# b, k and v of the RWKV pairs turned by VectorE and block moves instead of TensorE, the inverses' blocks packed, and row buffers taken later

## The chip, the cores and the metric

The kernel runs on one core of a Trainium2 chip. The metric is the device time of one execution in microseconds (us), as the median of several runs. A core has TensorE (PE in the profile; its weight loads are PEld), VectorE (DVE), ScalarE (ACT), GpSimd (POOL), SyncE (SP), which here issues every transfer, and 16 DMA engines.

## What is computed

One step of a hybrid decoder layer, for 1024 prompt tokens and 8 single-token samples with their own states, in float32:

```python
p = x @ w_in                                   # 1024 -> 9344 columns: GLA, RWKV, gates
p_gla, p_rwkv, p_gate = split(p)
o_gla, S_gla = gla_chunked(q, k, v, log_a)     # 4 heads, gated linear attention
pr = p_rwkv + (previous_token(p_rwkv) - p_rwkv) * mu
r, kb, vb, g_b, w_lr, aa_lr = split(pr)
...
# RWKV-7, 16 heads of 64, token after token:
S = S * w_t + (S @ -kk_t) (kk_t * a_t)^T + v_t k_t^T ;  y_t = S r_t
...
m = sigmoid(gate_a) * (o_gla @ w_up_gla) + sigmoid(gate_b) * (o_rwkv @ w_up_rwkv)
y = layernorm(ALPHA * x + m @ w_out)
```

The outputs are `y` for both groups and the new states.

## The kernel before

**Passes and blocks.** The tokens are worked in two passes: pass 0 has 512 prompt tokens and the 8 samples (two tiles of 260 columns), pass 1 the other 512 (one tile). Every projection is a list of blocks of 128 output columns. A block is 8 steps over the inner dimension, and each step three matmuls in a reduced format, with `x` and the weights split in a high and a low part (`xh`, `xl`, `whi`, `wlo`), added up in a PSUM bank of the group `proj` (two banks). In pass 0 the weights are loaded (`wraw`), split by ScalarE and an elementwise engine, and the parts are written to DRAM (`wh`, `wl`); pass 1 reads the parts back. `whi` and `wlo` have four buffers of half a block each, so there is room for the block at work and one more.

**Pairs.** The RWKV heads are worked in eight pairs per pass, 16 in all. Time is cut in `NCH` = 8 chunks of `C` = 64 tokens. Of a pair:

- `front` computes decays and the chunk's factors: `BK` (b and k, two heads by 64 tokens, for each chunk; a buffer of the group `wide`), `AZ` (a and r), and by matmul `GG`, the masked products of each chunk, whose part `GG[..., 0, h, ...]` is a strictly lower triangular 64 x 64 matrix per head.
- Each such matrix has an inverse that is built from 32 x 32 blocks. The diagonal blocks go to DRAM (`LD`) and come back with one matrix per partition (`L`, in a `wide` buffer); 31 pairs of VectorE operations solve them in `X`; they go to DRAM (`XD`) and back as blocks (`XT`).
- `back` computes the off-diagonal block: `X1` = `XT`'s first block transposed on VectorE, `pA` = `GG` x `X1`, copied to `As`, `pZ` = `As` x `XT`, copied to `XT`. Both are eight matmuls, one per chunk, on 128 x 128 weights with 64 columns, in float32, which the profile shows as two instructions each. Then `AZ` is copied into `GG`.
- `turn` transposes `BK` (eight 128 x 128 transposes on TensorE, four to a bank, each bank copied back over `BK`) and `v` (four, copied in four parts to `u`, which takes over `L`'s buffer). In the profile these are `big<-cons,wide` and `big<-cons,row`, since they run as matmuls with the identity in `cons`.
- `chain` goes through the 8 chunks one after the other, four dependent matmuls each, and `norm` finishes the pair.

There are buffers for two pairs at a time (`az`, `gg`, `XT` two each, `wide` four).

**Rows.** Results of a block go to a row buffer ([128, 520], 26 of them, the group `row`). In `blocks`, `evac = yield from b.act()` takes the row before the block's first matmul; the function it returns empties the bank later.

**Order.** The whole program is written out by a planner (`Order.run`): each piece of work is a stream, every operation has a price and a planned start, and at each step the operation with the smallest planned start less its stream's priority is issued. Each engine then runs its own list in that order; SP's list is one queue for all transfers. Streams of the kind `turn` have priority 0.5, those of the weights 0.3, and 0.6 more while no split weights are ready.

All operations are issued from one line of the planner's helper, line 215, so the profile tells them apart by their buffers: `big<-X,gg` is `pA`, `big<-XT,As` is `pZ`, `proj<-xh,whi` a projection.

Of the kernel before, what the change touches and what calls it, by code (L numbers as in the profile page):

```python
# [20 lines left out]
P = 128  # L21
# [28 lines left out]
    "sto": ([P, P], 1), "bnd": ([P, 1], 3), "st": ([P, 32], 3), "part": ([P, HALF], 2), "l2p": ([P, 2 * P], 2),  # L50
    "pair": ([P, 2, HT // 32], 3),
}
PARTS = ("part", "l2p")
# [349 lines left out]
class Kern(Order):  # L403
# [71 lines left out]
    def setup(self):  # L475
# [149 lines left out]
    def load_w(self):  # L625

        H = NK // 2
        todo = [(b.src, b.c0, j, b.c.i) for b in self.plan if b.src is not None for j in range(2)]
        raws, his, los, kept = [], [], [], {}

        def keep(src, c0, j, hi, lo):
            for v, x in zip("hl", (hi, lo)):
                t = self.dr.tile([P, 512], F32, name=f"w{v}{c0}_{j}")
                kept.setdefault((c0, j), []).append(t)
                yield self.S.dma_start(t, x.bitcast(F32))

        def high():
            n = 0
            while True:
                yield lambda: len(raws) > n  # L640
                hi = yield from self.get("whi")
                yield self.A.copy(hi, raws[n][0])
                his.append(hi)
                n += 1
                if n == count:
                    return

        def low():
            for n in range(count):
                yield lambda: len(his) > n  # L650
                lo = yield from self.get("wlo")
                raw, src, c0, j, i = raws[n]
                yield self.E.tensor_sub(lo, raw, his[n].bitcast(F32))
                self.free(raw)
                los.append(lo)
                if src is self.a["w_in"] and i == 0:
                    yield from keep(src, c0, j, his[n], lo)
                self.ws.append((his[n], lo))
            self.w_done = True
# [61 lines left out]
    def low_rank(self, c, raws, used):  # L721
# [26 lines left out]
            c.alr_ready += 1  # L748
        self.free(x_)

    def gla_row(self, c, rows, scale):
        x = yield from self.row(c.n, KEEP)
        rows.append(x)

        def ev(tt, t0, w, q):
            yield self.A.activation(x[:, t0:t0 + w], q, AF.Copy, scale=scale)
        return ev

# [177 lines left out]


    def lora(self, c):
        c.lraw = yield from self.row(c.n)
        return self.shift(c, 32, c.lraw, c.lraw[:, HT:])  # L940

    def lora_done(self, c):
        def parts():
# [40 lines left out]
    def shift(self, c, j, dst, smp):  # L984
# [4 lines left out]
        edge = {}  # L989

        def ev(tt, t0, n, q):
            np_ = n - c.ns if tt == last else n
            yield lambda: "pv" in self.has
            yield A.activation(dst[:, t0:t0 + n], q, AF.Copy, scale=omu)
            if tt < last:
# [12 lines left out]
                if not i:  # L1008
                    self.free(prev)
            if i == 0 and tt == last:  # L1010
                yield V.scalar_tensor_tensor(smp, self.shT[:, j], mu, dst[:, HT:c.n], ALU.mult, ALU.add)
        return ev

    def rwkv_row(self, c, rows, n, p):
        x = yield from self.row(c.n, KEEP)
        rows.append(x)
        return self.shift(c, 8 * n + p, x, self.smp[:, n, p])

    def pair(self, c, p, st, gate):
        d = SimpleNamespace()  # L1020
        yield lambda: len(self.idle["wide"]) > 1 and len(self.idle["az"]) > 0 and len(self.idle["gg"]) > 0 and c.fronts == p and c.lw_ready and "cst" in self.has
        yield from self.front(c, p, st, d)
        yield "turn"
        yield from self.back(d)
        yield from self.turn(d)
        yield "chain"
        yield lambda: self.chained == p - 1 + NPAIR * c.i
        yield from self.chain(c, p, d)
        self.chained += 1
        yield "norm"  # L1030
# [3 lines left out]
    def front(self, c, p, st, d):  # L1034
# [103 lines left out]
        d.AZ, d.BK, d.G, d.XT, d.v, d.bonus, d.pc, d.L = AZ, BK, GG, XT, st[2], st[1], pc, L_  # L1138
        d.y = Pc_[:, :HT]

    def back(self, d):
        GG, XT = d.G, d.XT

        X1_, As_ = (yield from self.get("X1")), (yield from self.get("As"))
        X1 = X1_.rearrange("p (c h t) -> p c h t", c=NCH, h=2)
        As = As_.rearrange("p (c h t) -> p c h t", c=NCH, h=2)
        q = [slice(32 * n, 32 * n + 32) for n in range(4)]
        for h in range(2):
            yield self.V.transpose(X1[q[2 * h], :, h], XT[q[2 * h], :, h, 0:32])
        pA = yield from self.bank("big", [P, NCH, 2, 32])  # L1150
        for x in range(NCH):
            yield self.P.matmul(pA[:, x], GG[:, x, 0], X1[:, x], start=True, stop=True)
        for h in range(2):
            yield self.C.copy(As[q[2 * h + 1], :, h, 0:32], pA[q[2 * h + 1], :, h])
        self.free(pA, X1_)
        pZ = yield from self.bank("big", [P, NCH, 2, 32])
        for x in range(NCH):
            yield self.P.matmul(pZ[:, x], As[:, x], XT[:, x, :, 32:64], start=True, stop=True)

        for h, hs in enumerate(HS):  # L1160
            yield self.C.copy(XT[q[2 * h], :, h, 32:64], pZ[q[2 * h], :, h])
            yield self.C.copy(GG[hs, :, 0, h], d.AZ[hs, :, 0, h])
        self.free(pZ, As_)

    def turn(self, d):

        for x in range(0, NCH, 4):
            pt = yield from self.bank("big", [P, 4, P])
            for n in range(4):
                yield self.tr(pt[:, n], d.BK[:, x + n])  # L1170
            yield self.C.copy(d.BK[:, x:x + 4], pt)
            self.free(pt)
        d.u = d.L.rearrange("p (c h v) -> p c h v", c=NCH, h=2)
        pt = yield from self.bank("big", [P, 4, P])
        for n in range(4):
            yield self.tr(pt[:, n], d.v[:, n * P:(n + 1) * P])
        self.free(d.v)
        for h in range(2):
            for n, hs in enumerate(HS):
                yield self.C.copy(d.u[HS[1 - h], n::2, h], pt[hs, :, h * C:h * C + C])  # L1180
        self.free(pt)

    def chain(self, c, p, d):
        A, V = self.A, self.V
# [171 lines left out]


    def gate_row(self, c, n, x):
        gt = yield from self.row(c.n, KEEP)

        def ev(tt, t0, w, q):
            yield self.A.copy(gt[:, t0:t0 + w], q)
            if tt == len(c.tiles) - 1:
                yield self.S.dma_start(self.sg[c.i][n][x], gt)
# [25 lines left out]
                    self.gts.append((gt, m))  # L1390

    def up_row(self, c, n, x):
        yield lambda: self.gts
        gt, m = self.gts.pop(0)

        def ev(tt, t0, w, q):
            s = slice(t0, t0 + w)
            yield self.V.tensor_mul(gt[:, s], q, gt[:, s])
            if n:
                yield self.E.tensor_add(gt[:, s], gt[:, s], m[:, s])  # L1400
# [189 lines left out]
    def run_all(self):  # L1590
# [4 lines left out]
        self.plan, self.xq, self.ws, self.wo, self.gts = [], [], [], [], []  # L1595
# [65 lines left out]
```

## Time and profile before

| what | us |
|---|---|
| median of three runs | 1655.22 |
| the runs | 1649.95, 1655.22, 1656.4 |
| span of the profiled execution, first to last instruction | 1647.8 |
| TensorE busy | 1604.5 (97%) |
| TensorE weight loads busy | 1422.9 (86%) |
| VectorE busy | 1234.7 (75%) |
| ScalarE busy | 844.6 (51%) |
| GpSimd busy | 103.3 (6%) |
| DMA engines, mean share of the span | 61.2% |

The profiled execution's whole device time isn't listed apart from the runs; its span is 2.2 us below the fastest of them and 7.4 below the median. How to read the rows: in groups of instructions, `out<-in` are the buffers, then partitions x elements, then the count; behind the first bar stand the busy time in us and the mean of one in ns, behind the second the idle time of the engine just before these instructions and what ended it. In a timeline the first column is the start, the second the duration, both in us. In the list of waits: the engine and what it wrote, `<-` what ended the wait, then us in total, times and the longest in us. SP's issues don't count as busy time. In rows by stage each engine has its busy time and instruction count, and the last three numbers are the granted TensorE clock, the DMA share and GB/s.

### The profile page before, as it was taken

The page shows a single profiled execution, that of the slowest core. Times are in us where ns is not written, and L with a number is a line of the kernel's source. Part 1 is how long each engine was busy: PE and PEld are TensorE (multiplying, and loading weights), DVE is VectorE, ACT ScalarE, POOL GpSimd, SP SyncE. Part 2 cuts the span into 40 slices and gives each one's busy share as a digit, 9 for nine tenths or more (in the row PEclk, how much of TensorE's full clock was granted, in tenths as well). Part 3 has the DMA queues.
Part 4 walks back from the last instruction along what each step waited for, and adds up shares of the span by engine and source line. Part 5 has one row for each costly group of instructions (what it writes and reads, how often), then busy time and mean ns, then how long its engine had stood idle before and what let it go on. Part 6 is the DMA issues. An engine that isn't in the chain of part 4 may idle for free.

```text
span 1647.8 us, 30094 instructions
## 1 busy us (share of the span) xinstructions
PE 1604.5 (97%) x10322; PEld 1422.9 (86%) x10322; DVE 1234.7 (75%) x3187; ACT 844.6 (51%) x2015; POOL 103.3 (6%) x192
## 2 busy tenths in 40 slices
PE   8999999999999999999999999999999999999998
PEld 7899999999999988788878787888788889988786
DVE  6787887788878887768678888796767775665565
ACT  5546755656476646553635462536345645554210
POOL 1100100100000000000001011100000000000000
PEclk9999999999999999999999999999999999999999
DMA  8878764696569655645465546544653577798432
GB/s 281 263 220 254 222 204 149 197 301 198 176 193 280 213 181 189 206 162 145 134 178 162 147 141 193 180 129 125 207 147 106 172 227 228 242 292 264 151 109 84
DMA packets 311925, 315.28 MB, mean 191 GB/s; under 512 B 75364, under 2 KB 197357, under 8 KB 311773
## 3 DMA queue, kind: packets, MB, share of 16 engines
q1 hardware_dynamic: 311772, 313.36, 61.2%
q8 instruction: 82, 1.34, 0.3%
q14 instruction: 71, 0.57, 0.1%
HBM read 195.45 MB, written 117.82 MB: 190 GB/s over the span
## 4 chain that ended last, share of the span: by engine, by line
PE 71%; DVE 13%; DMA 7%; ACT 3%; SPq 3%; issue 2%; POOL 0%; POOLq 0%; DVEq 0%; ACTq 0%
PE proj L215 39%; PE big L215 22%; PE pY L215 7%; PE pch L215 4%; DVE row L215 4%; SPq L215 3%; DVE X L215 2%; DVE Xt L215 2%; DMA wide<-LD 2%; ACT row L215 1%; DVE wide L215 1%; DVE wlo L215 1%; DVE pair L215 1%; DMA whi<-wh 1%; DMA l2s<-lora 1%
## 5 line engine op out<-in xcount | busy, mean ns | idle before, releaser
L215 PE MATMUL proj<-xh,whi 128*128 128x260 f32 (+1 forms) x1872 | 618.2, 330 | 0.1
L215 PE MATMUL proj<-xh,wlo 128*128 128x260 f32 (+1 forms) x1872 | 615.8, 329 | 0.5 <-POOL wlo L215 0.5
L215 PE MATMUL proj<-xl,whi 128*128 128x260 f32 (+1 forms) x1872 | 612.9, 327 | 0.8 <-DVE xl L215 0.7
L215 PEld LDWEIGHTS proj<-xh,wlo 128*128 128x128 f32 x1872 | 354.0, 189 | 28.0 <-issue 5.6
L215 PEld LDWEIGHTS proj<-xh,whi 128*128 128x128 f32 x1872 | 354.7, 189 | 24.7 <-issue 2.3
L215 PEld LDWEIGHTS proj<-xl,whi 128*128 128x128 f32 x1872 | 354.4, 189 | 24.8 <-issue 1.7
L215 ACT CAST whi<-wraw 128x512 fp32r<-128x512 f32 x210 | 130.1, 621 | 92.0 <-PE proj L215 42.3
L215 DVE TENSOR_TENSOR wlo<-wraw,whi 128x512 fp32r<-128x512 f32 x206 | 144.8, 706 | 42.1 <-ACT whi L215 37.3
L215 DVE TENSOR_TENSOR row<-row 128x512 f32<-128x512 f32 (+10 forms) x329 | 164.6, 505 | 11.5 <-PE big L215 4.5
L215 ACT ACTIVATE row<-row 128x512 f32<-128x512 f32 (+5 forms) x229 | 138.5, 610 | 33.2 <-DVE row L215 21.1
L215 ACT ACTIVATE row<-proj,omu 128x260 f32<-128x260 f32 (+1 forms) x99 | 54.2, 547 | 156.0 <-PE proj L215 155.6
L215 DVE TENSOR_TENSOR Xt<-X,wide 128x60 f32<-128x60 f32 (+24 forms) x496 | 108.7, 219 | 30.7 <-DMA wide<-LD 20.0
L215 PE MATMUL big<-row 128*128 128x64 f32 (+4 forms) x712 | 115.7, 281 | 6.5 <-DVE row L215 5.9
L215 DVE TENSOR_TENSOR X<-X,Xt 128x60 f32<-128x60 f32 (+24 forms) x496 | 107.4, 217 | 11.5
L215 ACT ACTIVATE s0p<-wide,pc 64x64 f32<-64x64 f32 x256 | 88.1, 344 | 43.4 <-DVE wide L215 39.1
L215 PEld LDWEIGHTS big<-row 128*128 128x128 f32 (+1 forms) x712 | 96.8, 191 | 15.5 <-DVE row L215 10.7
L215 DVE SCALAR_TENSOR_TENSOR wide<-pch,pc,s0p 64x64 f32<-64x64 f32 x224 | 63.1, 282 | 56.7 <-PE pch L215 52.2
L215 ACT COPY wide<-pch 64x64 f32<-64x64 f32 x230 | 47.3, 206 | 105.0 <-PE pch L215 101.6
L215 POOL TENSOR_TENSOR row<-row 128x512 f32<-128x512 f32 (+5 forms) x40 | 47.9, 1198 | 715.2 <-ACT row L215 210.8
L215 DVE SCALAR_TENSOR_TENSOR row<-proj,pv,row 128x259 f32<-128x259 f32 (+1 forms) x99 | 56.4, 570 | 40.5 <-ACT tail L215 23.7
L215 ACT COPY row<-big 128x128 f32<-128x128 f32 (+7 forms) x163 | 45.8, 307 | 52.4 <-PE big L215 51.3
L215 PE MATMUL big<-az,wide 128*128 128x256 f32 x256 | 66.7, 383 | 0.3 <-DVE gg L215 0.2
(256 smaller groups left out, 2714.5 us busy)
## 6 DMA issues: line engine op xcount, KB each, us to landing
wraw<-w_in SPq DMA_DIRECT2D x146, 256.0 KB
wh<-whi SPq DMA_DIRECT2D x146, 256.0 KB
wl<-wlo SPq DMA_DIRECT2D x146, 256.0 KB
whi<-wh SPq DMA_DIRECT2D x146, 256.0 KB
wlo<-wl SPq DMA_DIRECT2D x146, 256.0 KB
wide<-LD SPq DMA_DIRECT2D x64, 128.0 KB
wraw<-w_up_gla SPq DMA_DIRECT2D x32, 256.0 KB
wraw<-w_up_rwkv SPq DMA_DIRECT2D x32, 256.0 KB
```

The source lines that it names most:

```text
L215: ways.append((eng, lambda call=call: call(out, *args, **kw), price(eng, name, out, args, ins)))
```

## The change

- **b, k and v.** `turn` has no TensorE transposes any more. A new stream `turned`, started in `front` behind the `LD` and `Lp` transfers, transposes `v` and the two halves of `BK` in 32 x 32 blocks on VectorE into row buffers, frees `v`, writes the rows to DRAM (`VD`, `BD`), and reads `BD` back into `BK` in 16 block moves. `turn`, now ahead of `back`, reads `VD` into `u` in 8 moves. `chain` waits for `d.turned` as well, in the planner's order.
- **The inverses' blocks.** Four transfers gather the off-diagonal blocks of `GG` into `Lp`, in which four blocks stand on the diagonal of a 128 x 128 matrix; eight gather the solved blocks from `XD` into `Xs`. `back` then has four matmuls with 32 columns each for `pA` and for `pZ`, and eight copies of 32 partitions x 128 in place of four of 32 x 256.
- **Rows.** A block's row is taken by the new `landing`, in the function that empties the bank, with the first tile. `shift` gets a function `to` that is handed the row. `up_row` takes its place in the list `gts` at once and waits for the entry when it empties the bank.
- In `load_w` the line `los.append(lo)` moves behind the writes of the parts to DRAM.

```diff
+    "sto": ([P, P], 1), "Xs": ([P, 3 * P], 1), ...
+QS = tuple(slice(32 * n, 32 * n + 32) for n in range(4))
-        for tag, n, bufs in (("az", 4 * HT, 2), ("XT", 2 * HT, 2), ("X1", HT, 1), ("As", 2 * HT, 1)):
+        for tag, n, bufs in (("az", 4 * HT, 2), ("XT", 2 * HT, 2), ("Lp", HT, 1), ("As", HT, 1)):
...
-            evac = yield from b.act()
+            evac = b.act()
...
+    def landing(self, c, rows, tt):
+        if tt:
+            yield lambda: rows[0] is not None
+        else:
+            rows[0] = yield from self.row(c.n, KEEP)
+        return rows[0]
...
+        yield from self.turn(d)
         yield from self.back(d)
-        yield from self.turn(d)
         yield "chain"
-        yield lambda: self.chained == p - 1 + NPAIR * c.i
+        yield lambda: d.turned and self.chained == p - 1 + NPAIR * c.i
...
+        Lp = (yield from self.get("Lp")).rearrange("p (y t) -> p y t", t=P)
+        for n, b in enumerate(QS):
+            h = n % 2
+            yield self.S.dma_start(Lp[b, :, b], GG[QS[2 * h], n // 2::2, 0, h, 32:64])
+        VD = self.dr.tile([P, HT], F32, name=f"VD{c.i}{p}")
+        def turned():
+            BD = self.dr.tile([P, 2 * HT], F32, name=f"BD{c.i}{p}")
+            t = yield from self.row(HT)
+            yield V.transpose(t, v)
+            self.free(v)
+            yield self.S.dma_start(VD, t)
+            self.free(t)
+            for hf in range(2):
+                s = slice(hf * HT, hf * HT + HT)
+                t = yield from self.row(HT)
+                yield V.transpose(t, BK_[:, s])
+                yield self.S.dma_start(BD[:, s], t)
+                self.free(t)
+            src = BD.rearrange("(n a) (x q f) -> n q a x f", n=4, q=4, f=32)
+            for n, bn in enumerate(QS):
+                for q, bq in enumerate(QS):
+                    yield self.S.dma_start(BK[bq, :, bn], src[n, q])
+            d.turned = True
+        d.turned = False
+        self.spawn(turned(), "turn")
...
+        Xs = yield from self.get("Xs")
+        xp = Xs[:, :2 * P].rearrange("p (q y t) -> p q y t", q=2, t=32)
+        for n, b in enumerate(QS):
+            for q in range(2):
+                u = (2 * q + n % 2) * NCH + n // 2
+                yield self.S.dma_start(xp[b, q], XD[u:(2 * q + n % 2 + 1) * NCH:2].rearrange("c s t -> s c t"))
...
     def back(self, d):
-        for h in range(2):
-            yield self.V.transpose(X1[q[2 * h], :, h], XT[q[2 * h], :, h, 0:32])
-        for x in range(NCH):
-            yield self.P.matmul(pA[:, x], GG[:, x, 0], X1[:, x], start=True, stop=True)
...
+        yield self.V.transpose(d.Xs[:, 2 * P:3 * P], d.Xs[:, 0:P])
+        pA = yield from self.bank("big", [P, NCH // 2, 32])
+        for y in range(NCH // 2):
+            yield self.P.matmul(pA[:, y], d.Lp[:, y], X1[:, y], start=True, stop=True)
+        for b in QS:
+            yield self.C.copy(As[b, :, b], pA[b])
...
+        for y in range(NCH // 2):
+            yield self.P.matmul(pZ[:, y], As[:, y], X2[:, y], start=True, stop=True)
+        for n, b in enumerate(QS):
+            yield self.C.copy(XT[QS[2 * (n % 2)], n // 2::2, n % 2, 32:64], pZ[b])
...
     def turn(self, d):
-        for x in range(0, NCH, 4):
-            pt = yield from self.bank("big", [P, 4, P])
-            for n in range(4):
-                yield self.tr(pt[:, n], d.BK[:, x + n])
-            yield self.C.copy(d.BK[:, x:x + 4], pt)
-        for n in range(4):
-            yield self.tr(pt[:, n], d.v[:, n * P:(n + 1) * P])
...
+        src = d.VD.rearrange("(h n a) (x q f) -> h n q a x f", h=2, n=2, q=2, f=32)
         for h in range(2):
+            for n in range(2):
+                for q in range(2):
+                    yield self.S.dma_start(d.u[QS[2 - 2 * h + q], :, h, 32 * n:32 * n + 32], src[h, n, q])
```

More of the change, by code (lines that the diff above doesn't have):

```diff
@@ L49 @@
     "Xt": ([P, P], 1), "S": ([P, GDV], 2), "s0p": ([P, C], 2), "rh": ([P, P], 2),
-    "sto": ([P, P], 1), "bnd": ([P, 1], 3), "st": ([P, 32], 3), "part": ([P, HALF], 2), "l2p": ([P, 2 * P], 2),
+    "sto": ([P, P], 1), "Xs": ([P, 3 * P], 1), "bnd": ([P, 1], 3), "st": ([P, 32], 3), "part": ([P, HALF], 2), "l2p": ([P, 2 * P], 2),
     "pair": ([P, 2, HT // 32], 3),
@@ L749, in low_rank @@
         self.free(x_)
+    def landing(self, c, rows, tt):
[4 more added lines that the diff above has]
+        return rows[0]
     def gla_row(self, c, rows, scale):
-        x = yield from self.row(c.n, KEEP)
-        rows.append(x)
+        at = [None]
         def ev(tt, t0, w, q):
+            x = yield from self.landing(c, at, tt)
+            if not tt:
+                rows.append(x)
             yield self.A.activation(x[:, t0:t0 + w], q, AF.Copy, scale=scale)
@@ L938, in lora, with to @@
     def lora(self, c):
-        c.lraw = yield from self.row(c.n)
-        return self.shift(c, 32, c.lraw, c.lraw[:, HT:])
+        def to(x):
+            c.lraw = x
+        return self.shift(c, 32, to, None)
     def lora_done(self, c):
@@ L988, in shift @@
         last = len(c.tiles) - 1
-        edge = {}
+        edge, at = {}, [None]
         def ev(tt, t0, n, q):
             np_ = n - c.ns if tt == last else n
+            dst = yield from self.landing(c, at, tt)
+            if not tt:
+                to(dst)
             yield lambda: "pv" in self.has
@@ L1010, in ev @@
             if i == 0 and tt == last:
-                yield V.scalar_tensor_tensor(smp, self.shT[:, j], mu, dst[:, HT:c.n], ALU.mult, ALU.add)
+                yield V.scalar_tensor_tensor(dst[:, HT:c.n] if smp is None else smp, self.shT[:, j], mu, dst[:, HT:c.n],
+                                             ALU.mult, ALU.add)
         return ev
     def rwkv_row(self, c, rows, n, p):
-        x = yield from self.row(c.n, KEEP)
-        rows.append(x)
-        return self.shift(c, 8 * n + p, x, self.smp[:, n, p])
+        return self.shift(c, 8 * n + p, rows.append, self.smp[:, n, p])
     def pair(self, c, p, st, gate):
@@ L1142, in back @@
         GG, XT = d.G, d.XT
[L1144 to L1147, printed above, removed]
-        for h in range(2):
-            yield self.V.transpose(X1[q[2 * h], :, h], XT[q[2 * h], :, h, 0:32])
-        pA = yield from self.bank("big", [P, NCH, 2, 32])
-        for x in range(NCH):
-            yield self.P.matmul(pA[:, x], GG[:, x, 0], X1[:, x], start=True, stop=True)
@@ L1153, in back @@
-        for h in range(2):
[L1154 to L1162, printed above, removed]
@@ L1163, in back @@
-        self.free(pZ, As_)
-    def turn(self, d):
-        for x in range(0, NCH, 4):
-            pt = yield from self.bank("big", [P, 4, P])
-            for n in range(4):
-                yield self.tr(pt[:, n], d.BK[:, x + n])
-            yield self.C.copy(d.BK[:, x:x + 4], pt)
-            self.free(pt)
-        d.u = d.L.rearrange("p (c h v) -> p c h v", c=NCH, h=2)
-        pt = yield from self.bank("big", [P, 4, P])
-        for n in range(4):
-            yield self.tr(pt[:, n], d.v[:, n * P:(n + 1) * P])
[L1177 to L1181, printed above, removed]
+        As_ = yield from self.get("As")
@@ new lines, in back @@
+        As = As_.rearrange("p (y t) -> p y t", t=P)
+        X1, X2 = (d.Xs[:, n * P:(n + 1) * P].rearrange("p (y t) -> p y t", t=32) for n in (2, 1))
+        yield self.V.transpose(d.Xs[:, 2 * P:3 * P], d.Xs[:, 0:P])
[4 more added lines that the diff above has]
+            yield self.C.copy(As[b, :, b], pA[b])
+        self.free(pA, d.Lp)
@@ new lines, in back, with turn @@
+        pZ = yield from self.bank("big", [P, NCH // 2, 32])
+        for y in range(NCH // 2):
+            yield self.P.matmul(pZ[:, y], As[:, y], X2[:, y], start=True, stop=True)
+        for n, b in enumerate(QS):
+            h = n % 2
+            yield self.C.copy(XT[QS[2 * h], n // 2::2, h, 32:64], pZ[b])
+        for h, hs in enumerate(HS):
+            yield self.C.copy(GG[hs, :, 0, h], d.AZ[hs, :, 0, h])
+        self.free(pZ, As_, d.Xs)
+    def turn(self, d):
+        d.u = d.L.rearrange("p (c h v) -> p c h v", c=NCH, h=2)
+        src = d.VD.rearrange("(h n a) (x q f) -> h n q a x f", h=2, n=2, q=2, f=32)
+        for h in range(2):
+            for n in range(2):
+                for q in range(2):
+                    yield self.S.dma_start(d.u[QS[2 - 2 * h + q], :, h, 32 * n:32 * n + 32], src[h, n, q])
@@ L1358, in gate_row @@
     def gate_row(self, c, n, x):
-        gt = yield from self.row(c.n, KEEP)
+        at = [None]
         def ev(tt, t0, w, q):
+            gt = yield from self.landing(c, at, tt)
             yield self.A.copy(gt[:, t0:t0 + w], q)
@@ L1392, in up_row @@
     def up_row(self, c, n, x):
-        yield lambda: self.gts
-        gt, m = self.gts.pop(0)
+        place = len(self.asked)
+        self.asked.append(x)
         def ev(tt, t0, w, q):
             s = slice(t0, t0 + w)
+            yield lambda: len(self.gts) > place
+            gt, m = self.gts[place]
             yield self.V.tensor_mul(gt[:, s], q, gt[:, s])
```

7 lines of the change are left out of this document (4 added, 3 removed).

## The prediction

> **What bounds the kernel now.** I read the page first: engines, transfers, and the chain that ended last.
>
> ```profile
> span 1647.8 us, 30094 instructions
> PE 1604.5 (97%) x10322; PEld 1422.9 (86%) x10322; DVE 1234.7 (75%) x3187; ACT 844.6 (51%) x2015; POOL 103.3 (6%) x192
> DMA packets 311925, 315.28 MB, mean 191 GB/s; under 512 B 75364, under 2 KB 197357, under 8 KB 311773
> q1 hardware_dynamic: 311772, 313.36, 61.2%
> PE 71%; DVE 13%; DMA 7%; ACT 3%; SPq 3%; issue 2%; POOL 0%; POOLq 0%; DVEq 0%; ACTq 0%
> ```
>
> TensorE is busy for 97% of the span, which leaves 1647.8 - 1604.5 = 43.3 us in which nothing runs on it. VectorE has 413 us free, the 16 DMA engines 39% of the time. A busy TensorE need not be at its peak, so I looked next at the stages (engine times, clock, DMA share, GB/s; the first is pass 0, the second pass 1 of the row pairs, the third the output side), and at the starts of single matmuls.
>
> ```profile
> 0.00:625.00 625.00, 608.58 (x4781) 582.03 (x4782) 501.08 (x1358) 370.13 (x933) 44.34 (x94) 1.00 0.71 220
> 625.00:1300.00 675.00, 661.62 (x3663) 553.10 (x3662) 514.21 (x1404) 338.94 (x819) 54.24 (x89) 1.00 0.52 160
> 1300.00:1648.00 348.00, 334.31 (x1882) 287.77 (x1880) 219.39 (x425) 135.51 (x265) 4.72 (x9) 0.98 0.64 201
> ```
>
> In the two stages that hold the pairs TensorE idles 16.4 and 13.4 us, at the full clock. So there is hardly a wait to remove: what matters is how many microseconds of TensorE's own sequence the change takes out, and whether what replaces it puts waits in.
>
> The timeline of TensorE around the first pair's `back` and `turn` gives the prices. A printed duration includes the pipeline; the price is the distance between starts.
>
> ```profile
> 131.95 0.28 PE L215 MATMUL proj<-xl,whi 128*128 128x260 f32 x1
> 132.07 1.89 PE L215 MATMUL big<-X,gg 128*128 128x64 f32 x16
> 133.77 0.37 PE L215 MATMUL proj<-xh,wlo 128*128 128x260 f32 x1
> 133.97 0.28 PE L215 MATMUL proj<-xh,whi 128*128 128x260 f32 x1
> ...
> 137.43 0.60 PE L215 MATMUL big<-cons,wide 128*128 128x128 f32 x4
> ```
> ```profile
> 139.43 0.60 PE L215 MATMUL big<-cons,wide 128*128 128x128 f32 x4
> 139.86 0.60 PE L215 MATMUL big<-cons,row 128*128 128x128 f32 x4
> 140.22 0.36 PE L215 MATMUL proj<-xh,whi 128*128 128x260 f32 x1
> 140.42 0.28 PE L215 MATMUL proj<-xl,whi 128*128 128x260 f32 x1
> ...
> 141.96 0.51 PE L215 MATMUL big<-row 128*128 128x8 f32 x4
> 142.32 0.37 PE L215 MATMUL proj<-xh,whi 128*128 128x260 f32 x1
> ```
>
> Projection matmuls of 260 columns follow one another every 0.12 us (131.95 to 132.07). The 16 instructions of `pA` (each of the 8 matmuls runs as two) push the projection from 132.07 to 133.77, 1.70 us, and 0.08 more is lost on the way back (0.20 instead of 0.12). That is 0.106 us each. The row with 8 columns pays the same: four in 142.32 - 141.96 = 0.36 us and the 0.08 of the way back, 0.11 each. So a matmul of few columns isn't cheaper for having 32 columns in place of 64; only fewer of them save. Eight transposes take 140.42 - 139.43 - 0.12 = 0.87 us, 0.109 each.
>
> **The change part by part.**
>
> *Transposes leave TensorE.* 12 per pair (8 for b and k, 4 for v) x 0.109 = 1.31 us; 16 pairs: **-20.9 us**, on the path, since TensorE goes straight on with projections.
>
> *`back` packed.* `pA` and `pZ` go from 8 matmuls to 4 each, 16 instructions to 8: 2 x 8 x 0.106 = 1.70 us per pair, **-27.2 us** in all. If 32 columns were cheaper than the 8-column row says, it would be a little more; less is excluded by that row, since the matmuls still have the same 128 x 128 weights.
>
> *VectorE and ScalarE* (mean ns of one, before the second bar):
>
> ```profile
> L215 DVE STREAM_TRANSPOSE row<-row 128x512 f32<-128x512 f32 x16 | 11.3, 705 | 0.0
> L215 DVE STREAM_TRANSPOSE X<-XT 32x256 f32<-32x256 f32 x32 | 13.8, 431 | 2.5 <-DMA XT<-XD 2.0
> L215 ACT COPY wide<-big 128x512 f32<-128x512 f32 x31 | 18.2, 586 | 13.8 <-PE big L215 13.5
> L215 ACT COPY wide<-big 64x256 f32<-64x256 f32 x63 | 23.1, 366 | 1.6 <-PE big L215 0.8
> L215 ACT COPY row<-big 128x128 f32<-128x128 f32 x64 | 14.1, 270 | 18.4 <-PE big L215 18.4
> ```
>
> VectorE gains three transposes of 128 x 512 (3 x 0.705) and one of 128 x 128 (between 0.2, a quarter, and 0.43; I take 0.25) and loses two of 0.431: +1.50 us per pair, 24 us in all, to 1259 of some 1612 us, 78%. Copies out of PSUM lost per pair: 2 x 0.586, 4 x 0.366 and in `back` four of as many columns, 256; new are eight of 32 x 128, at most 0.27 each: -1.9 us, mostly ScalarE's. Both at nothing: the cover is TensorE's 97%. Without that cover VectorE's 24 us would show.
>
> *Transfers.* Per pair SP issues 4 (`Lp`) + 1 (`VD`) + 2 (`BD`) + 16 (`BK`) + 8 (`Xs`) + 8 (`u`) = 39 more. All but the three DRAM writes move pieces of 32 numbers, 128 B: 512 + 4096 + 1024 + 2048 = 7680 packets. The nearest rows are the moves that are there already, `XT` from `XD`: the tile's issues (min/median/max ns), the microsecond from 946 to 947, with nearly nothing but such packets in it, and SP's waits.
>
> ```profile
> L215 SPq DMA_DIRECT2D XT<-XD x64: 303/448/1873, 124.9 to 1365.4; - x64
> ```
> ```profile
> DMA packets 1063, 0.15 MB, mean 150 GB/s; under 512 B 1051, under 2 KB 1051, under 8 KB 1063
> ```
> ```profile
> SPq L215 <- PE proj L215: 270.9, 134, 7.3
> SPq L215 <- ACT whi L215: 99.6, 49, 9.6
> ...
> SPq L215 <- DMA LD<-gg: 7.1, 7, 2.1
> ...
> SPq L215 <- DMA XD<-X: 5.1, 10, 1.3
> ```
>
> Issues: 39 x 0.45 = 17.5 us of SP per pair, 281 in all; the two longest waits of SP alone come to 370 us, so the queue has room on average. Bytes: that microsecond moved 1051 small packets; at this rate 7680 take 7.3 us, and the three writes of 256 KB at the run's mean 191 GB/s 4.1 us: 11.4 us per pair at most. Pass 0: 0.71 x 625 = 444, plus 91, over 601 us: 0.89. Pass 1: 351 + 91 over 651: 0.68. So pass 0 comes near the ceiling. That this alone stalls nothing I read from a stage that is there already, with 0.85 and an idle time of 0.69 us:
>
> ```profile
> 1400.00:1500.00 100.00, 99.31 (x619) 88.44 (x618) 65.31 (x122) 55.52 (x104) 0.00 (x0) 1.00 0.85 268
> ```
>
> The queue is in order, so a read-back that waits for its write holds up the weight loads behind it (`wraw`, `whi`, `wlo`), for which TensorE waits in turn. Today two read-backs per pair (`LD`, `XD`) cost SP 7.1 + 5.1 = 12.2 us of waiting in the whole run. The change adds two more (`BD` to `BK`, `VD` to `u`). I take **+12.2 us**, as if all of it reached TensorE. Bounds: 0 (weights far enough ahead), and 67 us (worked out below as a rival).
>
> *`v` freed earlier, rows taken at the emptying.* Before, a block took its row buffer ahead of its first matmul. Could TensorE have waited for it?
>
> ```profile
> L215 PE MATMUL proj<-xh,whi 128*128 128x260 f32 x1256 | 365.3, 291 | 0.1
> L215 PE MATMUL proj<-xh,wlo 128*128 128x260 f32 x1256 | 364.3, 290 | 0.5 <-POOL wlo L215 0.5
> L215 PE MATMUL proj<-xl,whi 128*128 128x260 f32 x1256 | 362.8, 289 | 0.8 <-DVE xl L215 0.7
> ```
>
> The idle time in front of the projections is 1.4 us in all, so an earlier start is worth 1.4 at best; a row that is late now holds a bank of the two instead, after 24 x 0.12 = 2.9 us of further matmuls. A one-off stall of that size is the loss end. I take 0.
>
> *What is late next.* Behind the inverse the old path was: `X1` transposed at 130.8, chain's first matmul at 143.2.
>
> ```profile
> L215 DVE STREAM_TRANSPOSE X<-XT x32: 422/434/437, 130.8 to 1368.8; 32x256 f32<-32x256 f32 x32
> ```
> ```profile
> L215 PE MATMUL pch<-wide,gg x256: 270/275/377, 143.2 to 1417.0; 128*128 128x128 f32 x128
> ```
>
> The new path has 8 `Xs` and 8 `u` issues behind `XT`'s (7.2 us) and one landing (`XT`'s last issue started at 126.9 by its row, used at 130.8: 3.5 us after its end), and loses the stretch from the first transposes to the chain (137.43 to 143.2, 5.8 us): +4.9 us per pair. Cover: two sets of buffers, so the next pair's front and the projections run meanwhile. I cost it at nothing.
>
> **Sum.** -20.9 - 27.2 + 12.2 = -35.9: a span of 1611.9. The median of the runs, 1655.2, stands 7.4 us above the profiled span (the fastest, 1650.0, stands 2.2 above); with 7.4 the forecast is **1619 us**.
>
> **The rivals.**
>
> *A. The SP queue makes weights late (slower).* `turned` issues 19 transfers, 8.6 us, and `Xs` with `u` 16, 7.2 us. A block of weights lasts 48 x 0.12 = 5.8 us. If each burst goes out in one piece between two weight loads, TensorE stands 2.8 + 1.4 = 4.2 us per pair, 67 us in all: 1655 - 48 + 67 = 1674. It decides from 48.1 / 16 = 3.0 us per pair on. For it: in-order queue, 0.89 of the engines in pass 0. Against: SP's many waits for TensorE, which are gaps that moves can fill, and the stage at 0.85.
>
> *B. The pair's own path sets the rhythm (no change).* If the 4.9 us show on every pair of pass 1, where the projections are fewest for each microsecond of VectorE's work, 8 x 4.9 = 39 come back: 1655 - 48 + 39 = 1646, with the 12.2 beside it 1658. Against: TensorE's idle of 13.4 us in that stage. The Trainium skill (DMA: Bandwidth & Descriptors, the two cost components of a DMA) gives a fixed cost of about 2.0 us in place of the 3.5 that the row shows; by it, as an estimate, the path would grow by 3.4 us and B would come out at 1634. The row has other traffic in it, which the page's figure has not; I keep the row.
>
> *C. VectorE becomes the bound.* Its 24 us show in full: 1643. Against: 78%; for: it is the second on the chain, with 13%. The Trainium skill (VectorE: DVE Perf Modes, Rules for kernel authors) speaks against this change: a 128 x 128 transpose belongs on TensorE where PSUM will do as its target. By the rows above, 1.31 us of TensorE is indeed less than 2.1 us of VectorE and the moves; by that rule the edit loses wherever TensorE has slack, and this trace shows hardly any.
>
> *D. All of the gain and a little more.* No read-back reaches TensorE and fewer changes of matmul kind (three groups fewer per pair, 0.08 us each, 3.8 us): 1655 - 48 - 4 = 1603.
>
> **How the numbers follow.** Runs of this kernel differ by 0.4%, so about 0.5%, 8.3 us, can be told from no change. Chances: forecast 0.50, D 0.14, C 0.08 (faster); B 0.14, of which 0.08 lies within 8.3 us, 0.04 below and 0.02 above; A 0.14 (slower). Faster: 0.50 + 0.14 + 0.08 + 0.04 = 0.76; within: 0.08; slower: 0.14 + 0.02 = 0.16. The likeliest case's own range is 1603 to 1635. For 8 in 10 I leave A's upper part and a small tail below D out: 1598 to 1658.
>
> **What would show it.** Right: TensorE's instructions fall by 12 x 16 + 16 x 16 = 448, its busy time by some 45 us; `big<-cons,wide` is gone; SP has 624 more issues; packets under 512 B rise by some 123 thousand; VectorE is near 1259 us. Each step wrong: few-column matmuls of 32 columns at other than 0.106 us; TensorE waits ended by weights or by `SPq` (A); by the chain's `wide`, `XT` or `Xs` (B); by `row` on VectorE with VectorE above 90% (C). The prediction as a whole fails if TensorE's busy share falls well below 96%.

## The result, and the profile after

The changed kernel takes 1716.6 us (median; 1711.4 to 1718.3), the kernel before 1655.4: a ratio of 1.039, with an interval of 1.037 to 1.041. It is slower by 61 us, where 36 us of gain were forecast. The profiled execution's span is 1715.4 us, 67.6 more than before. The page (busy time by engine, the clock in 40 slices, the transfers):

```profile
span 1715.4 us, 29923 instructions
PE 1588.9 (93%) x9874; PEld 1393.7 (81%) x9874; DVE 1262.8 (74%) x3231; ACT 815.9 (48%) x1973; POOL 102.9 (6%) x192
PEclk9999999899999999999999999999999998999999
DMA packets 450934, 343.62 MB, mean 200 GB/s; under 512 B 208227, under 2 KB 330220, under 8 KB 450780
```

The 448 instructions have left TensorE as forecast (10322 to 9874), and 132.9 thousand small packets have come: the 122.9 forecast, and 10 thousand more, which is 16 for each of the 624 added transfers. But TensorE now idles for 1715.4 - 1588.9 = 126.5 us instead of 43.3, and its mean granted clock fell from 0.995 to 0.973. Counting a share of the clock that was not granted as lost time, 0.027 x 1715.4 = 46 us are lost to the clock instead of 8. So the 67.6 us are 83.2 of idle time and 38.1 of clock, less 53.7 of work that TensorE no longer has. This is an account and no measurement of that work: some 10 us of the clock loss, and 3 of it before, fall in time in which TensorE idled anyway and are counted twice. Counted by the trace only where TensorE was busy, the clock's part is 36.1 - 6.2 = 29.9 us, and the work that has left is 45.5. The three stages of the earlier view:

```profile
0.00:625.00 625.00, 583.60 (x4474) 555.58 (x4475) 488.89 (x1312) 347.63 (x890) 36.94 (x86) 0.98 0.79 236
625.00:1300.00 675.00, 621.25 (x3267) 507.68 (x3266) 518.46 (x1389) 305.54 (x747) 54.55 (x91) 0.98 0.60 175
1300.00:1716.00 416.00, 384.03 (x2138) 330.45 (x2137) 255.40 (x533) 162.77 (x337) 11.42 (x15) 0.96 0.60 187
```

In pass 1, where the transfer engines are only 0.60 busy, TensorE idles 53.8 us instead of 13.4; in pass 0, at 0.79, 41.4 instead of 16.4. So, by the averages, TensorE's waits don't go with full transfer engines. The groups say what it does wait for (last part: idle time before these instructions, and what ended most of it):

```profile
L216 PE MATMUL proj<-xh,whi 128*128 128x260 f32 (+1 forms) x1872 | 620.9, 332 | 38.6 <-DMA whi<-wh 26.7
L216 PE MATMUL proj<-xh,wlo 128*128 128x260 f32 (+1 forms) x1872 | 620.4, 331 | 3.6 <-DMA wlo<-wl 3.1
```

Before, 0.6 us in these two rows; now 42.2, and 29.8 of it ends with the landing of weights. One such wait, in SP's queue, on TensorE, and in stretches of 5 us (engine times, then the clock, the DMA share and GB/s):

```profile
774.97 0.43 SPq L216 DMA_DIRECT2D wlo<-wl  x1
...
775.97 0.56 SPq L216 DMA_DIRECT2D wide<-BD  x1
776.58 0.65 SPq L216 DMA_DIRECT2D sg<-row  x1
777.28 9.83 SPq L216 DMA_DIRECT2D wide<-BD  x13
787.21 0.54 SPq L216 DMA_DIRECT2D whi<-wh  x1
```
```profile
784.95 0.40 PE L216 MATMUL proj<-xh,wlo 128*128 128x512 f32 x1
790.48 0.80 PE L216 MATMUL proj<-xh,whi 128*128 128x512 f32 x1 [5.13 <-DMA whi<-wh]
791.07 0.63 PE L216 MATMUL proj<-xl,whi 128*128 128x512 f32 x1
791.50 0.63 PE L216 MATMUL proj<-xh,wlo 128*128 128x512 f32 x1
791.93 0.63 PE L216 MATMUL proj<-xh,whi 128*128 128x512 f32 x1
```
```profile
780.00:785.00 5.00, 5.00 (x23) 3.98 (x22) 4.35 (x20) 1.85 (x5) 0.00 (x0) 1.00 0.54 118
785.00:790.00 5.00, 0.35 (x2) 0.00 (x0) 4.48 (x20) 0.00 (x0) 0.00 (x0) 0.75 0.51 113
790.00:795.00 5.00, 4.52 (x12) 3.58 (x13) 0.85 (x3) 0.00 (x0) 0.00 (x0) 0.57 0.91 266
```

Thirteen moves of `BK` stand together in SP's queue, 9.83 us, 0.76 each with the pauses between them. The next block's `whi` is issued behind them at 787.21 and has landed some 3 us later; TensorE has been without work since 785.4. Then it goes on at about half speed: 512 columns every 0.43 us instead of 0.233, the granted clock 0.57 in this stretch. Meanwhile the transfer engines are half idle (0.54, 0.51). This is rival A, with a second price that no rival had.

The queue's own waits point the same way. In the prediction's row SP waited 134 times, 270.9 us in all, for TensorE to free a buffer of weights. In the changed kernel it does so half as often, as it would if it came to these loads when the buffer was already free:

```profile
SPq L216 <- PE proj L216: 131.2, 70, 7.2
```

The Trainium skill (TensorE: Matmul & The Clock Gate, Part 1) says that the clock is halved after an idle window of about 3.4 us and stays so for at least such a window of activity. The stretches above agree in the halving, but not in the time before it. A clock of 0.75 from 785 to 790 is half speed from about 787.5 on, some 2.2 us after the last matmul, and the last section shows a half-clock stretch behind a pause of 1.80 us. Here the measurement decides.

### The profile page after: what moved, and what is told of

The parts are those of the page before. It is cut to its first block, busy times and chain, and to the rows that moved or that the text cites. A ratio compares the mean times of both kernels' runs of the same rounds, so it can differ in the third digit from the quotient of the medians.

```text
span 1715.4 us, 29923 instructions
## 1 busy us (share of the span) xinstructions
PE 1588.9 (93%) x9874; PEld 1393.7 (81%) x9874; DVE 1262.8 (74%) x3231; ACT 815.9 (48%) x1973; POOL 102.9 (6%) x192
## 5 line engine op out<-in xcount | busy, mean ns | idle before, releaser
L216 PEld LDWEIGHTS proj<-xh,wlo 128*128 128x128 f32 x1872 | 357.8, 191 | 35.2 <-DMA wlo<-wl 11.0
L216 DVE TENSOR_TENSOR wlo<-wraw,whi 128x512 fp32r<-128x512 f32 x202 | 140.0, 695 | 73.5 <-ACT whi L216 66.3
L216 DVE TENSOR_TENSOR row<-row 128x512 f32<-128x512 f32 (+7 forms) x331 | 163.7, 500 | 21.5 <-ACT row L216 8.0
L216 ACT ACTIVATE row<-row 128x512 f32<-128x512 f32 (+4 forms) x229 | 138.2, 610 | 39.9 <-DVE row L216 20.6
L216 ACT COPY row<-big 128x128 f32<-128x128 f32 (+8 forms) x153 | 43.4, 310 | 70.7 <-PE big L216 69.4
L216 PE MATMUL big<-az,wide 128*128 128x256 f32 x256 | 71.0, 403 | 2.5 <-ACT As L216 1.3
```

Source lines behind the costliest of these rows:

```text
L216: ways.append((eng, lambda call=call: call(out, *args, **kw), price(eng, name, out, args, ins)))
```

## The experiments

Theory 1: SP's one in-order queue is the cost; each issue takes time there and weights come late behind it. Theory 2: the packets of 128 B fill the transfer engines. Theory 3: the later taking of rows and the other order of the plan. The tables' columns are the time and its ratio to the kernel before on the same chip, the issues on SP and their durations added up from the trace, TensorE's idle time (span less busy), and the clock loss worked out as above, so that a part of it falls in idle time. The kernel before took 1646 to 1655 us from series to series; between kernels of different series the ratios are the safer comparison.

| kernel | us | ratio (interval) | SP issues, us | idle | clock |
|---|---|---|---|---|---|
| before (profile) | 1655.4 | | 1461, 658 | 43 | 8 |
| changed | 1716.6 | 1.039 (1.037 to 1.041) | 2085, 1076 | 127 | 46 |
| e1_rows | 1650.7 | 1.001 (1.000 to 1.003) | 1461, 658 | 46 | 8 |
| e2_turn | 1706.0 | 1.035 (1.032 to 1.038) | 1893, 950 | 96 | 41 |
| e3_pack | 1651.4 | 1.002 (1.000 to 1.004) | 1653, 776 | 61 | 23 |
| e4_turn_pack | 1765.9 | 1.071 (1.067 to 1.074) | 2085, 1064 | 141 | 88 |
| e5_few_bytes | 1679.4 | 1.018 (1.015 to 1.020) | 2085, 983 | 90 | 44 |
| e6_merged | 1685.9 | 1.023 (1.019 to 1.028) | 1893, 982 | 97 | 45 |
| e7_pool_queue | 1626.2 | 0.986 (0.983 to 0.989) | 1461, 674 | 63 | 24 |
| e8_price | 1887.8 | 1.145 (1.141 to 1.148) | 2085, 1050 | 209 | 167 |
| e9_extra | 1714.6 | 1.041 (1.038 to 1.045) | 1845, 865 | 83 | 33 |
| e10_low | 1680.4 | 1.022 (1.017 to 1.026) | 2085, 1062 | 98 | 30 |
| e11_pool_merged | 1642.4 | 0.999 (0.996 to 1.001) | 1461, 674 | 75 | 33 |
| e12_pool_more | 1628.7 | 0.989 (0.986 to 0.991) | 1205, 544 | 64 | 19 |
| e13_no_rows | 1785.9 | 1.085 (1.081 to 1.088) | 2085, 1065 | 150 | 93 |
| e14_price52 | 1724.2 | 1.046 (1.044 to 1.049) | 2085, 1071 | 127 | 55 |
| e15_pool_price | 1645.6 | 0.997 (0.995 to 0.999) | 1461, 672 | 75 | 33 |

**The parts, one by one.** `e1_rows` is the kernel before with `landing` and what goes with it; `e2_turn` with `turned` and the new `turn`; `e3_pack` with `Lp`, `Xs` and the new `back`; `e4_turn_pack` with both of these.

> The kernel before, with the third part of the change alone (rows taken when the bank is emptied, up_row's place in the list, the moved line in load_w). No transfer is added. Theory 1 (SP's in-order queue): the loss comes from the 624 added issues, so this run is within 10 us of before, 1645 to 1665. Theory 2 (the 128-byte packets fill the transfer engines): the same, 1645 to 1665. Theory 3 (the rows and the other order of the plan do the harm): at least 1685, half of the loss.

> The kernel before, with the turning of b, k and v alone: 27 of the 39 added issues per pair, 6144 of the 7680 small packets, and 20.9 us less on TensorE. The whole change lost 61 us where 48 were saved on TensorE, so 109 us went elsewhere. Theory 1, by issues: 109 x 27/39 = 75, so 1655 - 21 + 75 = 1710. Theory 2, by packets: 109 x 6144/7680 = 87, so 1721. Theory 3: 1634, as TensorE's saving says.

> The kernel before, with the packing of the inverses' blocks alone: 12 added issues per pair, 1536 small packets, and 27.2 us less on TensorE. Theory 1, by issues: 109 x 12/39 = 34, so 1655 - 27 + 34 = 1662; if the queue only costs when it is full, below 1640. Theory 2, by packets: 22, so 1650. Theory 3: 1628.

> The changed kernel without the third part: rows taken before the block's first matmul, as before. All 39 issues and 7680 packets per pair stay. Theories 1 and 2: 1700 to 1730, as the whole change. Theory 3: near 1607 to 1630.

Rows alone do nothing, so theory 3 has no cost to show by itself. The kernel before took 1648.1 us in this series, 7 less than the expectations assume. Taken from there, turning alone was expected at 1703 by issues and 1714 by packets, and took 1706; packing alone at 1655 and 1643, and took 1651. Theory 3's numbers are missed by both; the other two aren't told apart yet. The fourth run came out above every expectation. It also lacked the moved line of `load_w`, without which the last weights of pass 0 and the first of pass 1 can change places; the amount of work is the same. So it was run again with that line:

```diff
-            evac = b.act()
+            evac = yield from b.act()
```

> The changed kernel with rows taken before the block's first matmul, as before, and the moved line of load_w kept (the first run of this kind lacked it, so that the last weights of pass 0 and the first of pass 1 could change places). If the rows part takes loss away when the queue is full: 1740 to 1775, as that run showed (1766). If that run's time came from the changed places: 1705 to 1725.

```profile
span 1779.3 us, 29916 instructions
...
PE 1629.5 (92%) x9874; PEld 1427.5 (80%) x9874; DVE 1264.6 (71%) x3236; ACT 815.5 (46%) x1965; POOL 102.2 (6%) x197
...
PEclk9999999999799989998798999999999988999999
```

1785.9: the page of this run shows 149.7 us of idling and a clock of 0.948. So with the queue full the kernel with the third part is 69 us faster (76 by the ratios), though alone this part is worth nothing. Whether the rows do that, or the other order of the plan that comes with them, isn't shown.

**Packets or time in the queue.** `e5_few_bytes` keeps every issue and moves one chunk of eight; `e6_merged` keeps every packet and has fewer issues:

```diff
-                    yield self.S.dma_start(BK[bq, :, bn], src[n, q])
+                    yield self.S.dma_start(BK[bq, 0:1, bn], src[n, q][:, 0:1])      # e5, and u alike
...
+            src = BD.rearrange("(n a) (x q f) -> q a x n f", n=4, q=4, f=32)        # e6
+            for q, bq in enumerate(QS):
+                yield self.S.dma_start(BK[bq].rearrange("a x (n f) -> a x n f", f=32), src[q])
```

> The changed kernel with all its issues, but the 16 moves of BK and the 8 of u carry one chunk of eight: 2304 small packets per pair in place of 7680. The other chunks of BK are set to zero by GpSimd and those of u are left as they were, so the output differs. Theory 1 with a price by the issue alone: as the whole change, 1700 to 1725. Theory 2 (packets): 70% of the 109 us go, 1640. If the time of one issue itself falls with its packets, in between, and the mean issue of these moves falls below 0.45 us.

> The changed kernel with the 16 moves of BK in 4 transfers of 1024 packets each: 27 added issues per pair in place of 39, the same packets and bytes. Theory 1: 109 x 12/39 = 34 us come back, 1683. Theory 2: no change, 1717. If an issue's time goes by its packets, the four take as long as the sixteen and the time stays near 1717.

The issues of `BK`'s moves (min/median/max ns, first and last start us) in the changed kernel, then in the two:

```profile
L216 SPq DMA_DIRECT2D wide<-BD x256: 542/607/1628, 89.0 to 1395.9; - x128
```
```profile
L216 SPq DMA_DIRECT2D wide<-BD x256: 302/419/1542, 90.0 to 1364.1; - x128
```
```profile
L216 SPq DMA_DIRECT2D wide<-BD x64: 562/688/3203, 90.6 to 1375.0; - x64
```

Both land within 7 us of each other. One has 30% of the added small packets and all issues, the other all packets and 27 of 39 issues; what they have alike is the time in SP's queue, 983 and 982 us. For these moves an issue's time falls with its packets (607 to 419 ns), which would be how fewer packets help. That fits theory 1 in the form that time counts, not number: `e5`'s 1700 to 1725, for a price by the issue alone, is missed, and so are theory 2's 1640 and 1717. The 31 and 37 us that come back are not far above what another order of the plan can do by itself (below), so these two runs alone would be an indication and no proof.

**The disputed cost by itself.** `e9_extra` has nothing of the change, only transfers that nobody reads:

```diff
+                    yield self.S.dma_start(EX[q, n].rearrange("x a f -> a x f"),
+                                           self.lev[bq].rearrange("a (x f) -> a x f", f=32))   # 24 per pair
```

> The kernel before with nothing of the change, but with 24 added transfers per pair at the place where the change issues its moves and with the same priority in the plan: 256 packets of 128 B each, from a constant to DRAM, that nobody waits for. Theory 1 (SP's in-order queue): 109 x 24/39 = 67 us are lost, 1700 to 1725, with TensorE's idle time and the half clock up as in the changed kernel. If the loss needs the read-backs or the pair's longer path, no change, 1645 to 1665.

```profile
span 1711.2 us, 30462 instructions
...
PE 1627.8 (95%) x10322; PEld 1436.8 (84%) x10322; DVE 1245.4 (73%) x3194; ACT 839.8 (49%) x1997; POOL 118.3 (7%) x205
```

68 us lost against 67 forecast, with no read-back of the added transfers and no added step in a pair's path. By the packet, as in `e2` with as many, 87 would have gone. The pairs' older transfers can still come late behind the added ones: TensorE's waits for VectorE's `X` are 15.7 us here, 0.5 before. Idle time is 83.4 instead of 43.3, the clock 0.981. The same can be asked of all runs: idle time and clock loss above those of before, by the time added to SP's queue. Changed kernel (83.2 + 38.1) / 417 = 0.29; turning 85 / 291 = 0.29; packing 33 / 118 = 0.28; `e5` 82 / 325 = 0.25; `e6` 91 / 323 = 0.28; `e9` 64 / 206 = 0.31. So in these six kernels each microsecond added to SP goes with a loss of 0.25 to 0.31 us. It isn't a constant: with nearly the SP time of the changed kernel and another order it is 0.19 in `e10`, 0.32 in `e14`, 0.44 in `e4`, 0.47 in `e13` and 0.83 in `e8`. And the four kernels with the moves on GpSimd (next) lose 32 to 57 us by the same account, though SP's time is at most 16 us above that of before. That part of the loss isn't SP's time.

**Another queue, another order.** `e7_pool_queue` issues the 39 from GpSimd; `e11` has four moves of `BK` there, `e12` the older small moves there too. `e10_low` leaves all on SP and lowers the moves' priority (`yield "out"` ahead of them).

> The changed kernel with the 39 added transfers of each pair issued from GpSimd's queue in place of SP's; the same packets. GpSimd is busy for 6%. Theory 1: SP's queue is as before, the 109 us go: 1607 to 1640. Theory 2: the packets still fill the engines, 1700 to 1717. Slower than 1717 if GpSimd's own issues take several us each, so that the moves come late for the chain.

> The changed kernel, all transfers on SP, but the 16 moves of BK have a priority in the plan below that of the weights (-0.1 in place of 0.5). Theory 1, with the burst of moves ahead of the weights as the cause: the plan puts weights first, 1660 to 1695. If the sum of SP's time counts and not its order, 1705 to 1725. Later moves may make the chain wait: above 1717.

> The added transfers on GpSimd's queue, and the 16 moves of BK in 4 of 1024 packets. With GpSimd's queue 1626 was measured. If that queue still holds up some moves, 1605 to 1620; if what is left comes from elsewhere (the transfer engines, the half clock), 1620 to 1630.

> As the one with 4 moves of BK on GpSimd's queue, and the transfers LD, L, XD and XT that the kernel before has (16 per pair) on GpSimd's queue too, so that SP carries little but weights, rows and x. Theory 1 carried on: SP's 0.45 us x 16 per pair are taken from its queue, a few us faster than the merged one. If GpSimd's issues of these, which lie on the pair's own path, come later than SP's did, slower by up to 30 us.

```profile
span 1621.4 us, 30259 instructions
...
PE 1558.1 (96%) x9874; PEld 1381.4 (85%) x9874; DVE 1267.3 (78%) x3238; ACT 807.4 (50%) x1959; POOL 456.5 (28%) x819
```
```profile
L218 PE MATMUL proj<-xh,whi 128*128 128x260 f32 (+1 forms) x1880 | 619.5, 330 | 2.7 <-DVE row L218 1.4
L218 PE MATMUL proj<-xh,wlo 128*128 128x260 f32 (+1 forms) x1880 | 619.4, 329 | 0.5 <-POOL wlo L218 0.5
```

With the same transfers on GpSimd's queue 90 us come back (87 by the ratios), and the kernel is 1.4% faster than before. In these two rows TensorE waits 3.2 us instead of 42.2, and no landing of weights stands there any more. SP waits for TensorE's buffers nearly as before, 129 times:

```profile
SPq L218 <- PE proj L218: 266.3, 129, 7.4
```

The expectation is wrong in one thing: the packets are not the same. The queues of the changed kernel, then of `e7` (packets, MB, share of the 16 engines):

```profile
q1 hardware_dynamic: 450780, 341.71, 66.4%
```
```profile
q1 hardware_dynamic: 311772, 313.36, 62.4%
q0 software_dynamic: 22272, 28.35, 6.6%
```

The bytes are the same, in far fewer packets. But the transfer engines were busy for nearly as long, 0.664 x 1715.4 = 1139 us there and 0.69 x 1621.4 = 1119 here. So the 90 us didn't come from emptier transfer engines, and theory 2 is missed in this form too.

GpSimd's issues show as busy time (456.5), 584 ns at the median by the tile's row. `e12`, with 115 us less in SP's queue than before, is faster than `e11` but not than `e7`, and `e11` lies above both of its ranges. The Trainium skill (DMA: Bandwidth & Descriptors, Rules for kernel authors) says that spreading transfers over the issuing engines doesn't add bandwidth and saves only issue time; here taking the issues off SP brings back most of the loss, 87 of some 109 us. Priority alone brings 36 us (28 by the ratios) with SP's time nearly the same (1062 us), so the order in the queue counts beside its sum.

**How much is the plan's order.** A changed price changes the whole order.

> The changed kernel with one number of the planner changed: a transfer's issue is planned at 0.65 us in place of 0.48, so the plan knows that SP is fuller. Theory 1: the planner moves weight loads ahead, and part of the loss comes back, 1670 to 1705. Theory 2: no change, 1705 to 1725.

> The changed kernel with a transfer planned at 0.52 us on SP, near the mean issue that the trace shows, 1075.5 / 2085 = 0.516, in place of 0.48. If the plan's wrong price makes the loss: 1660 to 1700. If the queue itself makes it: 1705 to 1735. With 0.65 it was 1888, so a plan that answers strongly to this price could also give more, up to 1780.

> The kernel with the added transfers on GpSimd's queue, planned at 0.5 us per issue in place of 0.7; nothing else differs, so the transfers and their queues are the same and only the order of the plan is another. The spread of the plan's order by itself: if small, 1620 to 1632 as with 0.7 (1626); if it is as large as between that run and the merged one (1642), 1610 to 1645.

`e8_price` went far the other way, to 1888. There TensorE waits for VectorE's results more than for weights: the planner, which took SP for fuller, wrote another and worse order:

```profile
PE big L216 <- DVE row L216: 58.1, 21, 11.7
PE big L216 <- DVE Xs L216: 32.0, 6, 13.3
...
PE proj L216 <- DMA whi<-wh: 5.3, 6, 1.6
```

The price near the measured one left the loss as it was (1724), so a wrong price isn't its cause. `e15` has the transfers of `e7` and is 19 us slower by the order alone. Hence the four kernels with moves on GpSimd (1626, 1629, 1642, 1646) show the return of 66 to 87 us by the ratios, and their distance to the kernel before, 0.1 to 1.4%, with an uncertainty of the plan's order as large. The same uncertainty lies on every single difference above, since each edit also changes the order of the plan.

## Why the prediction was wrong

- *TensorE's saving: right.* 48.1 us forecast, with 3.8 more in D; 45.5 to 53.7 by the account above. TensorE's busy time fell by only 15.6 us, where some 45 were to show, because the half clock lengthens what is left; its share fell to 93%, which the prediction named as its sign of failure. The eight instructions of `pA` with 32 columns take 144.01 - 143.06 = 0.95 us, forecast 0.85 and 0.08 for the change of kind:

```profile
143.06 0.97 PE L216 MATMUL big<-Xs,Lp 128*128 128x32 f32 x8
144.01 1.13 PE L216 MATMUL big<-az,wide 128*128 128x256 f32 x4
```

- *VectorE and ScalarE: right.* 1262.8 us against 1259; the 128 x 128 transpose took 305 ns, the small copies 256. Rival C is out: VectorE is at 74%.

```profile
L216 ACT COPY As<-big 32x128 f32<-32x128 f32 x62 | 15.9, 256 | 23.6 <-PE big L216 23.0
...
L216 DVE STREAM_TRANSPOSE Xs<-Xs 128x128 f32<-128x128 f32 x16 | 4.9, 305 | 0.1
```

- *The transfers: the step that failed.* The term of +12.2 us was sized from SP's two read-backs. In its place stand 113 to 121 us (83 idle, 30 to 38 clock); some 87 of them went away when the transfers left SP's queue, the rest stays open. Two readings were wrong. First, "the queue has room on average": SP's waits behind `PE proj` are not all room. There SP stands with a weight load in hand for the moment a buffer is freed, and a load that goes out later can be late for TensorE. Second, an issue was priced at 0.45 us from `XT`'s row, whose transfers have 256 small packets too; `BK`'s took 0.607 at the median, and 0.76 with the pauses in the burst shown. In sum SP's time grew by 417 us where 281 were forecast: 365 for the added transfers themselves, the rest because the older ones took longer. The bytes were no danger: DMA shares of 0.89 and 0.68 were forecast, 0.79 and 0.60 came.
- *Rival A, given a chance of 0.14: the mechanism right, the price half.* Its 67 us stand against 83 of idling, and the half clock after such waits, 30 to 38 us, was in no term: at 0.995 the kernel before hardly shows it. Its point of decision, 3.0 us per pair, was passed: 113 / 16 = 7.1 to 121 / 16 = 7.6 came.
- *From span to median:* 7.4 us were added, 1.2 came; too little to matter here.
- *Rows: 0 forecast, 0 alone.* That the kernel without them is 69 us slower when SP is full was not seen.
- *Rival B:* not shown as the cause: extra issues that add no step to a pair's path lose about as much for their time in the queue (`e9`). That pairs run late behind the queue is not ruled out as a part of the loss. The 2.0 us that the prediction sets beside its row is the Trainium skill's figure for transfers issued from GpSimd (DMA: Bandwidth & Descriptors, Anatomy of one DMA), while the row's are SP's. Here `BK`'s moves issued from GpSimd landed 4.8 us after their issue at the median (`e7`), among other traffic.

Partly open: which of the 83 us of added idling is a late weight and which a late `l2s`, `Xs` or row behind the same queue; only 29.8 us end with weights by the trace. When each pause of TensorE above 0.1 us is followed back through the trace to its start, a transfer or SP's queue stands in the chain of 73 of 118 us, against 11 of 35 before and 17 of 54 in `e7`. In `e9` it is only 28 of 75, so there the delay lies further back than the pauses. Open: why TensorE still idles 63 us with the moves on GpSimd, where before it idled 43, and why the plan with the price 0.65 is so much worse.

## What to carry to other kernels

Treat the issuing queue of transfers as an engine: add up its issue time, and ask of each of its waits whether it is spare or a load standing ready that must go out at that instant. In a kernel whose TensorE never stops, moves on another queue may cost little, while time put ahead of the weights costs part of itself and, behind pauses like those shown, a stretch at half clock on top. Price small-packet transfers by their issues before counting bytes, and try one in its own form: a row with as many packets gave 0.45 us, the moves themselves took 0.6.

## What the runs showed of the hardware that was not expected

An issue of `BK`'s moves on SP takes longer with more packets: 419 ns at the median for 32 packets of 128 B, 607 for 256, 688 for 1024 (but up to 3203), in the same place of the program. The number of packets isn't all of it: `e9`'s transfers have 256 of them too and took 449 ns. On GpSimd's queue the moves with 256 pieces took 584 ns, between 582 and 645, without SP's long tail (1628), and the profile counts far fewer packets for the same bytes.

```profile
L218 POOL DMA_DIRECT2D wide<-BD x256: 582/584/645, 89.5 to 1308.6; - x128
```

A pause of TensorE much shorter than 5 us can be followed by the half clock. In the changed kernel a pause of 1.80 us, with only one of 0.62 in the five us before it, is followed by 512 columns every 0.43 us, until 1060.35. By the trace's clock record the half-clock stretches of this run last 3.4 us, or 6.8, 10.2 or 13.7; the last, at the end, is 4.9:

```profile
1056.96 0.60 PE L216 MATMUL proj<-xh,whi 128*128 128x512 f32 x1 [1.80 <-DVE row L216]
1057.36 0.63 PE L216 MATMUL proj<-xl,whi 128*128 128x512 f32 x1
1057.79 0.63 PE L216 MATMUL proj<-xh,wlo 128*128 128x512 f32 x1
```
